# Low part of K on all 128 partitions, and a bfloat16 identity and mask, in the scores of a forgetting-attention layer

## The chip, the cores and the metric

One NeuronCore of one Trainium2 chip runs the whole program in one launch. The metric is the device time of that core in microseconds (us). Three runs of the kernel before gave a median of 2899.41 us (2898.84 to 2900.05).

## The reference, cut to what matters

A trunk of two layers over x of 1024 tokens by 1024 channels in float32: a short gated convolution beside a Mamba-2 scan, a convolutional FFN, a forgetting attention, and a second FFN, each followed by a layer norm. The change lies in the attention alone (16 heads of 64 channels, 1024 tokens):

```python
log_f = log_sigmoid(f_logit + b_f); cum = cumsum(log_f)
def block(q_blk, cum_blk, i):                 # 128 queries
    s = q_blk @ k.T * 64**-0.5 + cum_blk[..., None] - cum[:, :, None, :]
    s = where(key_pos <= qpos, s, -inf)
    p = softmax(s)
    return p @ v
```

## The kernel before, in words

Every float32 operand of a large product is held as the sum of two float32r parts, high and low, made by `split` (L95 to L98): ScalarE copies the high part, VectorE subtracts it from the source. A product takes three passes (high high, high low, low high).

`attention` (L520) handles the heads in eight pairs. The projections to q, k and v (`projections`, L610) run 24 units of 2 halves with 24 products of 512 columns each (L621), in steps of four products. Each finished half is evacuated beside the next one (`evacuations`, L572). For one head of a pair, q is a tile of 128 partitions: the high part of its 64 channels on one half of the partitions, the low part on the other (L603, L604). `kh` holds the high part of K on both halves (the split at L599 and the copy at L600), so that one product with 128 rows gives q high times k high plus q low times k high. `kl`, the low part of K, holds both heads of a pair in one tile, each on its own 64 partitions.

`scores` (L646) then makes, for 128 queries (tile i) and the (i + 1) * 128 keys up to them, in one accumulation in PSUM: the products with `kh` (128 rows), those with `kl` (64 rows), each in pieces of up to 512 keys, and one product of the identity with a mask that adds 1e38 above the diagonal (L660, 128 columns). VectorE adds the cumulated gates and takes the minimum (L663), ScalarE the exponential (L666), VectorE the reciprocal (L667), GpSimd the scaling (L668). `weigh` (L671) transposes the probabilities (L682) and splits them; `values` (L688) multiplies by v (L698), and adds the two halves of the result with a copy `ot` by ScalarE (L701) and an add by VectorE (L702).

The order: the loop at L771 goes over the 128 tiles of scores; the transposes follow two tiles, the values four tiles behind, and between them `fill` takes steps of the projections (and for the last pair, steps of the output projection, L729). Tile pools give each tag a number of slots: `kl` 2, `kh` 3, `q` 3, `vc` 1 (the copy of v before its transposes, L586, L589), `ot` 2. `places_of` (L746) names slots that come free at the end for parts of the output projection. The framework orders the instructions and places the waits.

Of the kernel before, what the change touches and what calls it, by code (L numbers as in the profile page):

```python
# [18 lines left out]
P = 128  # L19
L = 1024  # L20
# [9 lines left out]
LAG, VLAG = 2, 4    # tiles of 128 tokens by which the transposes and P @ V follow the scores  # L30
XLAG = 2            # tiles by which the transposes into x.T follow the layer norm
LEAD = 12           # steps by which the projections run ahead of the heads
FILL, FILL7 = 36, 72  # steps of products between the heads of a pair, and of the last pair


class Net:
    """The trunk. Every float32 operand of a large product is held as the exact sum of
    two float32r parts, high and low; a product takes the passes hh, hl and lh."""
# [56 lines left out]
    def split(self, high, low, src, engine=None):  # L95
        """high + low == src exactly."""
        self.nc.scalar.copy(high, src)  # L97
        (engine or self.nc.vector).tensor_sub(low, src, high.bitcast(F32))  # L98
# [19 lines left out]
    def project(self, *srcs):  # L118
        """[128 channels, L] = W[:, 128 channels].T @ x.T for each slice of W; several go
        side by side over the rows of x.T."""  # L120
        nc = self.nc
        ws = [src if isinstance(src, (tuple, list)) else self.weight(src) for src in srcs]
        ps = [self.mm_ps() for _ in srcs]
        steps = [(half, k, t, n) for k in range(KD) for t in range(len(srcs)) for n in range(3) for half in range(2)]
        if self.fresh > 0:
            self.fresh -= len(srcs)
            steps.sort(key=lambda s: s[0])
        for half, k, t, n in steps:
            if half:
                while self.after:  # L130
                    self.after.pop(0)()
            h, l = ws[t]
            w, x = ((h, self.xh), (h, self.xl), (l, self.xh))[n]
            hs = slice(half * 512, half * 512 + 512)
            nc.tensor.matmul(ps[t][:, hs], lhsT=w[:, k * P:(k + 1) * P], rhs=x[:, k, hs],  # L135
                             start=(k == 0 and n == 0), stop=(k == KD - 1 and n == 2))
        return ps if len(srcs) > 1 else ps[0]

    def conv(self, out, ps, w, bias=None):
        """Causal depthwise convolution along the free axis; w[:, K] by channel."""  # L140
        nc = self.nc
        K = w.shape[-1]
        if bias is None:
            nc.scalar.activation(out, ps, AF.Copy, scale=w[:, K - 1:K])
        else:
            nc.scalar.activation(out, ps, AF.Identity, scale=w[:, K - 1:K], bias=bias)  # L146
        for s in range(1, K):
            nc.vector.scalar_tensor_tensor(out=out[:, s:], in0=ps[:, :L - s], scalar=w[:, K - 1 - s:K - s],  # L148
                                           in1=out[:, s:], op0=ALU.mult, op1=ALU.add)

    def down(self, ys, ws, evac, late=0):
        """evac(i, psum) for each tile i of 128 tokens of y @ W; what it returns is called after the
        products of the next tile or, after the last tiles, beside the next projection. The last ones
        of ys may come late."""
        nc = self.nc
        n = len(ys)
        blocks = [range(3)] + [[i] for i in range(3, NT)] if late else [[i] for i in range(NT)]
        after = self.after
        for block in blocks:
            ps = {i: self.mm_ps() for i in block}  # L160
            for js in (range(n - late), range(n - late, n)):
                for i in block:
                    for j in js:
                        (yh, yl), (wh, wl) = ys[j], ws[j]
                        for m, (y, w) in enumerate(((yh, wh), (yh, wl), (yl, wh))):
                            for hs in (slice(0, 512), slice(512, D)):
                                nc.tensor.matmul(ps[i][:, hs], lhsT=y[:, i * P:(i + 1) * P], rhs=w[:, hs],  # L167
                                                 start=(j == 0 and m == 0), stop=(j == n - 1 and m == 2))
            while len(after) > XLAG - 1:
                after.pop(0)()  # L170
            after += [then for then in [evac(i, ps[i]) for i in block] if then]

    def log1p_exp_neg_abs(self, x, tmp):
        """log1p(exp(-|x|)) / 2, by 2 atanh(e / (2 + e))."""
# [19 lines left out]
    def thin_weight(self, src, into):  # L194
        """The 16 columns of W as the first of 128, the others zero."""
        nc = self.nc
        raw = self.wp.tile([P, KD, P], F32, tag="wraw", name="wraw", bufs=2)
        nc.gpsimd.memset(raw, 0.0)
        nc.sync.dma_start(raw[:, :, :NH], src)
        self.split(*into, raw.rearrange("p k c -> p (k c)"))  # L200
        return into

    def token_major_16(self, ps, t):
        """[128, (tile of 128 tokens, 16)] from [16 channels, L]; t: [128, L] of scratch."""
        nc = self.nc
        nc.scalar.copy(t[:NH], ps[:NH])
        tp = self.sm_ps()
        for i in range(NT):
            nc.tensor.transpose(tp[:, i * NH:(i + 1) * NH], t[:NH, i * P:(i + 1) * P], self.ident[:NH, :NH])
        return tp  # L210

# [7 lines left out]
    def layer_norm(self, r, ps, rsum, lg, lb, spare=None):  # L219
        """In place on r[128 tokens, D], with its sums over D; ps is free for scratch."""  # L220
# [74 lines left out]
    def mixer0(self):  # L295
# [17 lines left out]
        with ExitStack() as s1:  # L313
            cq = s1.enter_context(tc.tile_pool(name="cq", bufs=1))
            xs = [self.rp.tile([P, D], F32, tag=f"r{c}", name=f"xs{c}") for c in range(NT)]
            with ExitStack() as s2:
# [5 lines left out]
                # dt and the decays, [128 steps, chunk, head]  # L322
# [30 lines left out]
                # x, B, C  # L353
# [73 lines left out]
                # gated short convolution, with the scan beside it  # L427
# [14 lines left out]
            # gate  # L442
# [31 lines left out]
            # output projection  # L474
# [45 lines left out]
    def attention(self, r_in):  # L520
# [8 lines left out]
        with tc.tile_pool(name="fox", bufs=1) as fp:  # L529
# [7 lines left out]
            maskr = fp.tile([P, P], F32R, name="maskr")  # L537
            V.tensor_copy(maskr, mask)
            identr = fp.tile([P, P], F32R, name="identr")
            V.tensor_copy(identr, self.ident)  # L540
            # cumulative log forget gates
# [30 lines left out]
            def evacuations(pr, kind, n, ps):  # L572
                """Half n of the projection in its bank, as the operands of the heads 2 pr and 2 pr + 1."""
                h = half[n]
                if n == 0:
                    if kind == "v":
                        tiles["vc"] = fp.tile([P, L], F32, tag="vc", name="vc", bufs=1)
                        tiles[pr, "v"] = fp.tile([P, NT, 2, P], F32R, tag="v", name="v", bufs=2)
                    elif kind == "k":
                        tiles[pr, "kl"] = fp.tile([P, L], F32R, tag="kl", name="kl", bufs=2)  # L580
# [3 lines left out]
                if kind == "v":  # L584
                    vc, v = tiles["vc"], tiles[pr, "v"]
                    nc.scalar.copy(vc[:, h], ps)  # L586
                    yield
                    for c in range(4):
                        nc.tensor.transpose(ps[:, c * P:(c + 1) * P], vc[:, (4 * n + c) * P:(4 * n + c + 1) * P], self.ident)  # L589
# [6 lines left out]
                for e, (a, b) in enumerate(sides):  # L596
                    if kind == "k":
                        kh, kl = tiles[pr, "kh"][e], tiles[pr, "kl"]
                        self.split(kh[a, h], kl[a, h], ps[a])  # L599
                        nc.scalar.copy(kh[b, h], ps[a])  # L600
                    else:
# [8 lines left out]
            def projections():  # L610
                """All of q, k and v, in steps of a few products, each half evacuated beside the next."""
# [34 lines left out]
            def scores(pr, e, i):  # L646
                q, kh, kl = [tiles[pr, kind] for kind in ("q", "kh", "kl")]
                n = (i + 1) * P
                ts = slice(i * P, n)
                es = slice(e * 64, e * 64 + 64)  # L650
# [5 lines left out]
                for m, (a, k) in enumerate(((q[e], kh[e]), (q[e][es], kl[es]))):  # L656
                    for bs in parts:
                        nc.tensor.matmul(wide[:, bs], lhsT=a[:, ts], rhs=k[:, bs], start=(m == 0),  # L658
# [29 lines left out]
            def values(pr, e, g):  # L688
# [11 lines left out]
                ot = fp.tile([64, 256], F32, tag="ot", name="ot", bufs=2)  # L700
# [10 lines left out]
            def output_projection():  # L711
                """alpha x + o @ W of the heads 0 to 7 on x_d, in steps of a few products."""
# [33 lines left out]
            def places_of(j):  # L746
                """Slots for the parts of y and W of pair j that the last projections and heads leave free."""
# [4 lines left out]
                elif j == 5:  # L752
                    v = fp.tile([P, 2, L], F32R, tag="v", name="late", bufs=2)
                    t = [own("kl", 2), own("vc", 1), v[:, 0], v[:, 1]]
                elif j == 6:
                    t = [own("q", 3), own("kh", 3)] + weights()
                else:
                    t = [own("p", 4), own("p", 4), own("kl", 2), own("q", 3)]
# [34 lines left out]
            # the rest of the output projection  # L793
# [33 lines left out]
def _inputs(a):  # L827
    """The arrays as the chip reads them: tiles of 128 rows or columns, each contiguous."""
# [57 lines left out]
```

## Time and profile before

| | |
|---|---|
| median of 3 runs | 2899.41 us |
| span of the profiled execution, first to last instruction | 2901.4 us |
| PE busy | 2867.8 us (99%), 13378 matmuls |
| DVE busy | 1525.6 us (53%) |
| ACT busy | 918.5 us (32%) |
| POOL busy | 173.0 us (6%) |

PE is the matmul engine, PEld its weight loads, DVE VectorE, ACT ScalarE, POOL GpSimd. The page gives no other time of the profiled execution than its span; it lies 2.0 us above the median of the runs. Matmuls are pipelined and the end of each is modelled, so a matmul's duration holds more than the time by which it moves the next one; what a matmul takes of the engine is read here from the start of one to the start of the next.

### The profile page before, as it was taken

What the parts mean: (1) busy time and instruction counts of PE and PEld (TensorE: products, weight loads), DVE (VectorE), ACT (ScalarE), POOL (GpSimd) and SP (SyncE); (2) the same over time, 40 slices, a digit from 0 to 9 for tenths busy, and PEclk for the clock granted to TensorE, in tenths of its full rate; (3) what the DMA queues carried; (4) which work ended last, traced back from release to release, by engine and by line L of the source; (5) the groups of instructions that cost most, each with busy time, mean ns of one, the idle gap of its engine ahead of it and who ended that gap; (6) DMA issues with size and microseconds to landing.
All of it is one profiled execution on the core that took longest, in us unless ns stands there. A gap on an engine that the chain in (4) does not pass through costs nothing.

```text
span 2901.4 us, 32466 instructions
## 1 busy us (share of the span) xinstructions
PE 2867.8 (99%) x13378; PEld 2328.2 (80%) x13378; DVE 1525.6 (53%) x2085; ACT 918.5 (32%) x1346; POOL 173.0 (6%) x176
## 2 busy tenths in 40 slices
PE   8999999999999999999999999999899999999998
PEld 7888888888788888888887777777687888888887
DVE  4545564444644444554475555555575444444446
ACT  4521111321322222222235555555333222222222
POOL 0000000000000000000002222222100000000000
PEclk9999999999999999999999999999999999999999
DMA  3112221352011111111111111111532111111111
GB/s 136 44 66 81 75 78 66 131 189 87 22 51 56 57 48 51 51 44 44 59 73 53 52 52 44 45 44 51 182 124 73 44 44 44 51 52 57 51 37 73
DMA packets 56771, 194.50 MB, mean 67 GB/s; under 512 B 9392, under 2 KB 9776, under 8 KB 56624
## 3 DMA queue, kind: packets, MB, share of 16 engines
q1 hardware_dynamic: 56624, 192.44, 18.8%
q8 instruction: 105, 1.72, 0.2%
q14 instruction: 42, 0.34, 0.0%
HBM read 167.64 MB, written 24.77 MB: 66 GB/s over the span
## 4 chain that ended last, share of the span: by engine, by line
PE 91%; DVE 5%; ACT 1%; DMA 1%; issue 1%; POOL 0%; SPq 0%; POOLq 0%; ACTq 0%; DVEq 0%
PE mm L135 50%; PE mm L167 20%; PE mm L621 8%; PE mm L658 3%; PE sm L698 3%; PE sm L682 2%; PE mm L660 1%; PE sm L403 1%; PE mm L729 1%; DVE r L230 1%; DVE r L227 1%; DVE s L663 1%; ACT mm L226 1%; PE sm L414 0%; PE sm L409 0%
## 5 line engine op out<-in xcount | busy, mean ns | idle before, releaser
L135 PE MATMUL mm<-xh,wh 128*128 128x512 f32 x2112 | 667.7, 393 | 9.0 <-ACT xh L97 6.9
L135 PE MATMUL mm<-xh,wl 128*128 128x512 f32 x2112 | 663.0, 391 | 0.1
L135 PE MATMUL mm<-xl,wh 128*128 128x512 f32 x2112 | 661.4, 391 | 0.0
L98 DVE TENSOR_TENSOR wl<-wraw,wh 128x1024 fp32r<-128x1024 f32 x217 | 265.4, 1224 | 643.1 <-ACT wh L97 642.6
L97 ACT CAST wh<-wraw 128x1024 fp32r<-128x1024 f32 x217 | 228.0, 1051 | 1123.2 <-PE mm L135 927.3
L135 PEld LDWEIGHTS mm<-xh,wh 128*128 128x128 f32 x2112 | 395.6, 188 | 96.4 <-ACT xh L97 7.8
L135 PEld LDWEIGHTS mm<-xh,wl 128*128 128x128 f32 x2112 | 396.8, 188 | 86.2 <-issue 2.9
L135 PEld LDWEIGHTS mm<-xl,wh 128*128 128x128 f32 x2112 | 397.3, 188 | 84.8 <-issue 1.7
L282 DVE SCALAR_TENSOR_TENSOR r<-r,mm 128x1024 f32<-128x1024 f32 x160 | 195.0, 1219 | 134.1 <-PE mm L167 130.4
L167 PE MATMUL mm<-wh,yh 128*128 128x512 f32 x832 | 260.0, 392 | 0.3
L167 PE MATMUL mm<-wl,yh 128*128 128x512 f32 x832 | 256.8, 390 | 0.0
L167 PE MATMUL mm<-wh,yl 128*128 128x512 f32 x832 | 256.2, 389 | 0.0
L148 DVE SCALAR_TENSOR_TENSOR ug<-mm,ffn_cw,ug 128x1022 f32<-128x1022 f32 (+1 forms) x176 | 224.3, 1277 | 10.8 <-ACT ug L146 9.2
L167 PEld LDWEIGHTS mm<-wh,yh 128*128 128x128 f32 x832 | 153.9, 188 | 36.3 <-issue 5.1
L167 PEld LDWEIGHTS mm<-wh,yl 128*128 128x128 f32 x832 | 156.2, 188 | 32.7
L167 PEld LDWEIGHTS mm<-wl,yh 128*128 128x128 f32 x832 | 156.1, 188 | 32.6
L668 POOL TENSOR_TENSOR s<-s,sum 128x128 f32<-128x128 f32 (+7 forms) x128 | 147.8, 1155 | 459.0 <-DVE sum L667 412.0
L621 PE MATMUL mm<-xh,wh 128*128 128x512 f32 x384 | 159.1, 414 | 0.0
L621 PE MATMUL mm<-xh,wl 128*128 128x512 f32 x384 | 158.0, 412 | 0.0
L621 PE MATMUL mm<-xl,wh 128*128 128x512 f32 x384 | 154.4, 402 | 0.0
L663 DVE CUSTOM_DVE_ANT_0 s<-mm,cb 128x128 f32<-128x128 f32 (+7 forms) x128 | 96.5, 754 | 77.5 <-PE mm L660 61.1
L98 DVE TENSOR_TENSOR p<-sm,p 128x512 fp32r<-128x512 f32 (+1 forms) x192 | 105.5, 554 | 35.8 <-ACT p L97 33.9
(225 smaller groups left out, 2937.3 us busy)
## 6 DMA issues: line engine op xcount, KB each, us to landing
wraw<-in_ffn_w_up SPq DMA_DIRECT2D x88, 512.0 KB, 3.4
wraw<-in_sc_ssm_w_in SPq DMA_DIRECT2D x44, 512.0 KB, 3.5
wraw<-in_ffn_w_down SPq DMA_DIRECT2D x44, 512.0 KB, 3.4
wraw<-in_fox_w_in SPq DMA_DIRECT2D x24, 512.0 KB, 3.4
R<-acs_d SPq DMA_DIRECT2D x16, 512.0 KB, 3.6
wraw<-in_sc_ssm_w_out SPq DMA_DIRECT2D x16, 512.0 KB, 3.8
cb<-cum_d SPq DMA_DIRECT2D x16, 512.0 KB, 3.6
xraw<-in_xT SPq DMA_DIRECT2D x8, 512.0 KB, 9.3
```

The costliest lines, as they stand in the source:

```text
L97: self.nc.scalar.copy(high, src)
L98: (engine or self.nc.vector).tensor_sub(low, src, high.bitcast(F32))
L135: nc.tensor.matmul(ps[t][:, hs], lhsT=w[:, k * P:(k + 1) * P], rhs=x[:, k, hs], start=(k == 0 and n == 0), stop=(k == KD - 1 and n == 2))
L148: nc.vector.scalar_tensor_tensor(out=out[:, s:], in0=ps[:, :L - s], scalar=w[:, K - 1 - s:K - s], in1=out[:, s:], op0=ALU.mult, op1=ALU.add)
L167: nc.tensor.matmul(ps[i][:, hs], lhsT=y[:, i * P:(i + 1) * P], rhs=w[:, hs], start=(j == 0 and m == 0), stop=(j == n - 1 and m == 2))
L282: nc.vector.scalar_tensor_tensor(out=r[i], in0=r[i], scalar=ALPHA if first else 1.0, in1=ps, op0=ALU.mult, op1=ALU.add, **({"accum_out": r ...
L621: nc.tensor.matmul(place, lhsT=a[:, k * P:(k + 1) * P], rhs=x[:, k, half[n]], start=(m == 0), stop=(m == KD * 3 - 1))
L658: nc.tensor.matmul(wide[:, bs], lhsT=a[:, ts], rhs=k[:, bs], start=(m == 0), stop=(m == 1 and bs.stop < n))
L663: V.tensor_tensor_reduce(out=s[:, :n], in0=wide[:, :n], in1=cb[:, :n], op0=ALU.add, op1=ALU.min, scale=1.0, scalar=3e38, accum_out=mn)
L668: nc.gpsimd.tensor_tensor(s[:, :n], s[:, :n], sm.broadcast_to([P, n]), op=ALU.mult)
L682: nc.tensor.transpose(tp[:, c * P:(c + 1) * P], s[:, (b + c) * P:(b + c + 1) * P], self.ident)
L698: nc.tensor.matmul(ops[:, cs], lhsT=v[:, j, e, :], rhs=pt[j // 4 * 2 + m][:, j % 4, cs], start=(j == 0 and m == 0), stop=(j == 2 * g + 1 a ...
```

## The change

- `kl` becomes one tile for each head, with the low part on both halves of the partitions: the half with the head's channels is written as before, and a further ScalarE copy (64 partitions by 512) takes it to the other half. The product with it has 128 rows, with the same stationary q as that with `kh`. The tag has 3 slots in place of 2.
- The identity and the mask of the diagonal are bfloat16 in place of float32r.
- The copy of v before its transposes has 512 columns in place of 1024, and `ot` takes its slot (one slot for both, in place of one and two).
- `places_of` takes two `kl` slots for pair 5 (before: one and `vc`).

Comments and docstrings are also taken out.

```diff
-            maskr = fp.tile([P, P], F32R, name="maskr")
+            maskr = fp.tile([P, P], BF16, name="maskr")
-            identr = fp.tile([P, P], F32R, name="identr")
+            identr = fp.tile([P, P], BF16, name="identr")
...
-                        tiles["vc"] = fp.tile([P, L], F32, tag="vc", name="vc", bufs=1)
...
-                        tiles[pr, "kl"] = fp.tile([P, L], F32R, tag="kl", name="kl", bufs=2)
+                        tiles[pr, "kl"] = [fp.tile([P, L], F32R, tag="kl", name="kl", bufs=3) for _ in range(2)]
...
-                    vc, v = tiles["vc"], tiles[pr, "v"]
-                    nc.scalar.copy(vc[:, h], ps)
+                    vc, v = fp.tile([P, 512], F32, tag="vc", name="vc", bufs=1), tiles[pr, "v"]
+                    nc.scalar.copy(vc, ps)
...
-                        kh, kl = tiles[pr, "kh"][e], tiles[pr, "kl"]
+                        kh, kl = tiles[pr, "kh"][e], tiles[pr, "kl"][e]
                         self.split(kh[a, h], kl[a, h], ps[a])
                         nc.scalar.copy(kh[b, h], ps[a])
+                        nc.scalar.copy(kl[b, h], kl[a, h].bitcast(F32))
...
-                for m, (a, k) in enumerate(((q[e], kh[e]), (q[e][es], kl[es]))):
+                for m, k in enumerate((kh, kl)):
                     for bs in parts:
-                        nc.tensor.matmul(wide[:, bs], lhsT=a[:, ts], rhs=k[:, bs], start=(m == 0),
+                        nc.tensor.matmul(wide[:, bs], lhsT=q[:, ts], rhs=k[:, bs], start=(m == 0),
...
-                ot = fp.tile([64, 256], F32, tag="ot", name="ot", bufs=2)
+                ot = fp.tile([64, 256], F32, tag="vc", name="ot", bufs=1)
...
-                    t = [own("kl", 2), own("vc", 1), v[:, 0], v[:, 1]]
+                    t = [own("kl", 3), own("kl", 3), v[:, 0], v[:, 1]]
...
-                    t = [own("p", 4), own("p", 4), own("kl", 2), own("q", 3)]
+                    t = [own("p", 4), own("p", 4), own("kl", 3), own("q", 3)]
```

## Rows read from the trace of the kernel before

**Rows 1.** The page: span, and granted TensorE clock in 40 slices.
```profile
span 2901.4 us, 32466 instructions
...
PEclk9999999999999999999999999999999999999999
```

**Rows 2.** The chain that ended last, shares of the span by engine.
```profile
PE 91%; DVE 5%; ACT 1%; DMA 1%; issue 1%; POOL 0%; SPq 0%; POOLq 0%; ACTq 0%; DVEq 0%
```

**Rows 3.** Busy us (instructions) by engine, clock, DMA: one pair; late in the last.
```profile
1579.75:1648.33 68.58, 68.33 (x371) 53.22 (x370) 40.38 (x94) 39.62 (x84) 18.38 (x16) 1.00 0.14 47
...
2060.00:2080.00 20.00, 16.10 (x78) 12.16 (x77) 8.76 (x17) 4.62 (x8) 0.83 (x1) 1.00 0.67 212
```

**Rows 4.** PE in order of time over one head: start us, us, line, operation.
```profile
1705.48 0.22 PE L658 MATMUL mm<-kh,q 128*128 128x128 f32 x1
1705.63 0.32 PE L658 MATMUL mm<-kl,q 64*128 64x128 f32 x1
1705.88 0.33 PE L660 MATMUL mm<-maskr,identr 128*128 128x128 f32 x1
1706.04 0.45 PE L621 MATMUL mm<-xh,wh 128*128 128x512 f32 x1
1706.33 0.40 PE L621 MATMUL mm<-xl,wh 128*128 128x512 f32 x1
1706.56 0.40 PE L621 MATMUL mm<-xh,wl 128*128 128x512 f32 x1
...
1708.63 0.36 PE L658 MATMUL mm<-kh,q 128*128 128x256 f32 x1
...
1709.43 0.63 PE L682 MATMUL sm<-ident,s 128*128 128x128 f32 x4
...
1711.39 0.33 PE L658 MATMUL mm<-kh,q 128*128 128x384 f32 x1
1711.65 0.44 PE L658 MATMUL mm<-kl,q 64*128 64x384 f32 x1
1712.02 1.63 PE L698 MATMUL sm<-p,v 128*128 128x256 f32 x12
1713.48 0.27 PE L660 MATMUL mm<-maskr,identr 128*128 128x128 f32 x1
1713.59 0.30 PE L682 MATMUL sm<-ident,s 128*128 128x128 f32 x1
...
1714.66 0.40 PE L658 MATMUL mm<-kh,q 128*128 128x512 f32 x1
...
1715.58 0.41 PE L682 MATMUL sm<-ident,s 128*128 128x128 f32 x2
...
1719.56 0.45 PE L658 MATMUL mm<-kh,q 128*128 128x512 f32 x2
...
1720.59 0.51 PE L682 MATMUL sm<-ident,s 128*128 128x128 f32 x3
...
1733.26 0.62 PE L658 MATMUL mm<-kh,q 128*128 128x512 f32 x2
...
1734.64 0.62 PE L682 MATMUL sm<-ident,s 128*128 128x128 f32 x4
```

**Rows 5.** Weight loads in order of time, same stretch; idle time before in brackets.
```profile
1705.62 0.18 PEld L658 LDWEIGHTS mm<-kl,q 64*128 64x128 f32 x1 [0.19 <-issue]
...
1706.33 0.19 PEld L621 LDWEIGHTS mm<-xh,wl 128*128 128x128 f32 x1
```

**Rows 6.** The copy of K's high part (L600): ns min/median/max, first and last start.
```profile
L600 ACT CAST kh<-mm x32: 577/582/587, 1528.5 to 2011.9; 64x512 fp32r<-64x512 f32 x32
```

**Rows 7.** Waits from 1470 to 2110 us: total us, times, longest.
```profile
ACT kh L600 <- DVE kl L98: 18.7, 25, 1.4
...
PEld sm L698 <- DVE p L98: 8.4, 17, 1.6
```

**Rows 8.** The copies of tile ot, in the same columns.
```profile
L701 ACT COPY ot<-sm x64: 369/369/373, 1555.7 to 2121.0; 64x256 f32<-64x256 f32 x64
```

More of the change, by code (lines that the diff above doesn't have):

```diff
@@ L584, in evacuations @@
                 if kind == "v":
-                    vc, v = tiles["vc"], tiles[pr, "v"]
-                    nc.scalar.copy(vc[:, h], ps)
+                    vc, v = fp.tile([P, 512], F32, tag="vc", name="vc", bufs=1), tiles[pr, "v"]
+                    nc.scalar.copy(vc, ps)
                     yield
                     for c in range(4):
-                        nc.tensor.transpose(ps[:, c * P:(c + 1) * P], vc[:, (4 * n + c) * P:(4 * n + c + 1) * P], self.ident)
+                        nc.tensor.transpose(ps[:, c * P:(c + 1) * P], vc[:, c * P:(c + 1) * P], self.ident)
                     tv = ps.rearrange("p (c e d) -> p c e d", c=4, e=2)
@@ L646, in scores @@
             def scores(pr, e, i):
-                q, kh, kl = [tiles[pr, kind] for kind in ("q", "kh", "kl")]
+                q, kh, kl = [tiles[pr, kind][e] for kind in ("q", "kh", "kl")]
                 n = (i + 1) * P
                 ts = slice(i * P, n)
-                es = slice(e * 64, e * 64 + 64)
                 if i == 0:
```

## The prediction

> **What bounds the kernel now.** I read the page first, then the chain of waits, the busy time by stretch, and the matmul engine in order of time. The page shows a span of 2901.4 us and the clock at its upper level in nearly every slice [rows 1]. The chain of what ended last lies on PE for 91% of the span [rows 2]. In the attention, whose score tiles are all that the change touches, one pair of heads takes 68.58 us, PE is busy for 68.33 of them, and DVE and ACT for 40.38 and 39.62 [rows 3]. So in this stage any time by which PE gets on sooner shortens the kernel, until another engine's chain comes late; ACT has some 29 us a pair to spare. The exception is the last pair: late in it PE is busy for 16.10 of 20.00 us and the DMA engines for 0.67 of the time [rows 3]. There transfers set part of the pace.
>
> A matmul's worth has to be read from start to start. In the projections' stream one with 512 columns and 128 rows takes 0.23 us (1706.33 to 1706.56) [rows 4]. Its weight load does not add to that: the load for the matmul of 1706.56 starts at 1706.33, together with the matmul before it [rows 5]. With 256 columns the product with v takes about 0.12 us (twelve in 1.46 us, from 1712.02 to 1713.48, two of them of 128 columns) [rows 4]. I take 0.175 for 384 columns, half way, as an estimate. With 128 columns, the mask's product takes 0.11 us where it stands between products of 128 rows (1713.48 to 1713.59) [rows 4].
>
> **The change part by part.** *The product with K's low part on 128 rows.* Now it has 64 rows, and around it the steps are long. In tile 0 of the head shown, high part to low part takes 0.15 us, low part to mask 0.25, and mask to the next product 0.16, for three matmuls of 128 columns that cost 0.11 each elsewhere [rows 4]. The weight load of the low part starts at 1705.62, beside its own matmul and not beside the one before, after 0.19 us in which PEld waited for nothing that the profile shows [rows 5]. Going from 128 rows to 64 and back thus costs a stall on the way in and one on the way out. With all three products on 128 rows I expect the steps of the stream. For each tile, from the first product with the high part to the product behind the mask [rows 4]:
> - tile 0: 0.56 us now (1705.48 to 1706.04); three of 0.11 = 0.33 after; gains 0.23.
> - tile 1: 0.80 (1708.63 to 1709.43); 0.12 + 0.12 + 0.11 = 0.35; gains 0.45.
> - tile 2, where the products with v stand ahead of the mask: its two steps are 0.26 + 0.37 = 0.63; two of 0.175 = 0.35; gains 0.28. Its mask is already among products of 128 rows.
> - tile 3: 0.92 (1714.66 to 1715.58); 0.23 + 0.23 + 0.11 = 0.57; gains 0.35.
> - tile 4: 1.03 (1719.56 to 1720.59); 0.23 + 0.11 + 0.23 + 0.11 + 0.11 = 0.79; gains 0.24.
> - tile 7: 1.38 (1733.26 to 1734.64); four of 0.23 and 0.11 = 1.03; gains 0.35.
> - tiles 5 and 6 at the mean of tiles 4 and 7: 0.30 each.
>
> That is 2.50 us a head and 40.0 us for 16 heads. The first seven pairs give 35.0 us. Of the last pair's 5.0 us I count 3.5: its first head runs as the others do, but part of the second waits for transfers, and a wait for a transfer grows by what PE saves ahead of it.
>
> A rule of the Trainium skill speaks against part of this. The page "TensorE: Matmul & The Clock Gate", in Part 3 under "The mechanism", says that a weight load runs beside matmuls in flight only where the two use different row groups. By it the low part's products would go on paying for their loads on 128 rows; with the same page's time for a load of 128 columns, 107 ns ("LDWEIGHTS"), their 192 pieces would keep an estimated 20.5 us of the gain. The trace does not agree, since the projections' loads lie beside matmuls on the very same rows [rows 5].
>
> I keep the stream's step; what would come of the low part's loads staying in the open is rival 4.
>
> *Identity and mask as bfloat16.* No row shows a bfloat16 matmul. At best its step falls to 0.055 us, an estimate from the stream's slope (0.23 - 0.12 us for 256 columns more, half of it for 128) [rows 4]; that is 128 times 0.055 = 7 us more gain. At worst PE stalls when the type changes as it does now when the rows change: 0.25 + 0.16 us around the mask in tile 0 against 0.22 [rows 4], so 0.19 us a tile and 24 us of the gain back. I take the 0.11 us that the same product shows between others of 128 rows, the nearest row, since what follows it must load its weights all the same.
>
> *The further ScalarE copy.* There are 32 of them, like the copy at L600: 0.58 us each, 18.6 us in all, 2.3 us a pair [rows 6]. L600 already waits 18.7 us in 25 of its turns for VectorE's subtraction of the low part, which is just what the new copy reads [rows 7]; so the new one finds its data there. ACT would go from 39.6 of 68.6 us to about 42 of 64. At nothing, then, by ACT's free time. If that cover fails, up to 18.6 us come onto the path, since ACT works in order and the exponentials and the copies of the probabilities stand behind it. PE waits 8.4 us in 17 turns for VectorE's part of those probabilities today [rows 7]. I add 1 us to these waits and to those of the new slots.
>
> *Slots.* `kl` with three slots turns over like `kh`, for the same scores, so it adds no later release. `ot` and the copy of v now share one slot. `ot` is held for a copy of 0.37 us and an add, 64 times over 565 us, so about once in 9 us [rows 8]; 16 copies of v must find a place between them. Either can wait for the other for a microsecond or two on ACT; behind it stand the exponential and the probabilities of the next tiles. At nothing up to 16 times 1 us; I take it as part of the 1 us above. The late slots of pair 5 need the scores of head 14, which are done some tiles earlier; nothing.
>
> The sum: 35.0 + 3.5 - 1.0 = 37.5 us off a span of 2901.4, so 2863.9. The median of the runs lies 2.0 us under this span, so 2861.9, which I round to 2862.
>
> **The rivals.**
> 1. *The stall stays at the bfloat16 product.* PE stalls for the change of type on both sides of the mask. For it: the present stall sits just there, and nothing shows a mixed pair. Against: a float32 transpose follows the float32r mask at 0.11 us (1713.48 to 1713.59) [rows 4], though both are four bytes wide. The gain is 37.5 - 24 = 13.5 us: 2886.
> 2. *ACT comes late.* The copies are on the path for their whole length because PE now comes 7% sooner to whatever ACT makes. For it: values already wait for the probabilities [rows 7]. Against: ACT is free for 29 us of a pair [rows 3]. All 18.6 us lost: 2880.
> 3. *Slower.* Each evacuation of K holds ACT until VectorE's subtraction, queued behind its sum over the scores, and PE stands for the copy and the wait. It takes over 37.5 / 32 = 1.2 us of PE's time for each of 32 copies to decide so. At 0.58 for the copy [rows 6] and 1.4 for the wait, the longest that L600 has now [rows 7], it would be 63 us lost: 2925. Against: such waits exist now and PE misses only 0.25 us a pair [rows 3].
> 4. *Nothing.* The low part's loads stay in the open on 128 rows too. At 0.18 us each [rows 5], 192 of them take 35 us, and the gain of 37.5 shrinks to 2.5: about 2899. For it: they are in the open now. Against: the projections' loads are not [rows 5]. By the load time of the page named above it would be 17 us of gain, 2882.
>
> **How the numbers follow.** My forecast (gain of 33 to 47 us: 2852 to 2866) gets 0.70; rival 1 0.10, rival 2 with its half-way cases 0.12, rival 3 0.04, rival 4 0.04. The range takes the forecast, with the cheaper mask at its low end, and rival 2 up to its full price: 2851 to 2881, holding 0.82. A change under 0.2% (5.8 us) is about what a measurement here can't tell from none. Faster by more: the forecast and rivals 1 and 2, 0.92; within it: rival 4, 0.04; slower: rival 3, 0.04.
>
> **What would show it.** In the changed kernel's order of time, tile 3 of a head should take about 0.57 us from its first product to the one behind the mask, and tile 7 about 1.03; a pair about 63.5 us. Low part to mask at over 0.3 us in tile 3, or mask to next at 0.16, would show rival 1. More than 20 us of PE waiting for ACT or VectorE in the attention would show rivals 2 or 3. The low part's step at 0.33 us with 512 columns would show rival 4. I am wrong in the sum if the last pair takes all of its 5.0 us, or more, for transfers, or if the framework puts the products into another order.

## The result, and the profile after

The changed kernel takes 2856.89 us (median of 4 runs, 2855.09 to 2857.63) against 2899.26 us before: a ratio of 0.9851 with a 95% interval of 0.9837 to 0.9865, 42.4 us less. The forecast was 2862 us, 37.5 us less.

The page of the kernel after, with the lines that answer to [rows 1] and the table of busy times:

```profile
span 2853.1 us, 32454 instructions
...
PE 2818.5 (99%) x13378; PEld 2314.7 (81%) x13378; DVE 1525.8 (53%) x2085; ACT 934.5 (33%) x1378; POOL 173.0 (6%) x176
...
PEclk9999999999999999999999999999999999999999
```

As many matmuls as before; ACT has 32 instructions and 16.0 us more. Its four runs also show that a run's time is its span and 1.8 to 2.0 us more (2853.1 and 2855.09 in the profiled one).

The kernel after, busy us by engine in stretches as in [rows 3]: one pair; late in the last pair; and the whole last pair, from the mask of its first tile to its last product with v:

```profile
1593.46:1656.54 63.08, 62.52 (x371) 51.65 (x370) 40.25 (x94) 41.40 (x88) 18.35 (x16) 1.00 0.15 51
...
2014.00:2034.00 20.00, 17.99 (x90) 14.17 (x89) 9.88 (x17) 5.01 (x9) 0.65 (x1) 1.00 0.64 206
...
1974.40:2071.90 97.50, 90.06 (x499) 72.55 (x498) 62.42 (x119) 46.19 (x88) 19.85 (x17) 1.00 0.56 190
```

A pair went from 68.58 to 63.08 us, ACT in it from 39.62 to 41.40.

The kernel after, PE in order of time over a head, as in [rows 4] (the lines of the scores are L657 and L659 now, the transposes L681):

```profile
1690.61 0.22 PE L657 MATMUL mm<-kh,q 128*128 128x128 f32 x1
1690.67 0.28 PE L657 MATMUL mm<-kl,q 128*128 128x128 f32 x1
1690.78 0.23 PE L659 MATMUL mm<-maskr,identr 128*128 128x128 bf16 x1
1690.82 0.47 PE L621 MATMUL mm<-xh,wh 128*128 128x512 f32 x1
...
1693.44 0.37 PE L657 MATMUL mm<-kh,q 128*128 128x256 f32 x1
...
1693.81 0.48 PE L621 MATMUL mm<-xh,wl 128*128 128x512 f32 x1
1694.54 0.63 PE L681 MATMUL sm<-ident,s 128*128 128x128 f32 x4 [0.25 <-DVE p L98]
...
1699.17 0.40 PE L657 MATMUL mm<-kh,q 128*128 128x512 f32 x1
1699.41 0.39 PE L657 MATMUL mm<-kl,q 128*128 128x512 f32 x1
1699.64 0.23 PE L659 MATMUL mm<-maskr,identr 128*128 128x128 bf16 x1
1699.70 0.39 PE L681 MATMUL sm<-ident,s 128*128 128x128 f32 x2
...
1716.22 0.62 PE L657 MATMUL mm<-kh,q 128*128 128x512 f32 x2
...
1717.20 0.61 PE L681 MATMUL sm<-ident,s 128*128 128x128 f32 x4
```

Tile 0 takes 0.21 us where it took 0.56, tile 1 0.37 (0.80), tile 3 0.53 (0.92), tile 7 0.98 (1.38). The low part follows the high part at 0.06 us in tile 0 and 0.24 in tile 3, and the product behind the mask comes 0.04 to 0.06 us after it. New is a transpose that starts 0.73 us after the projection ahead of it (1693.81 to 1694.54), where a step is 0.23.

Weight loads of the kernel after, in order of time, as in [rows 5]:

```profile
1690.61 0.19 PEld L657 LDWEIGHTS mm<-kl,q 128*128 128x128 f32 x1
1690.78 0.10 PEld L659 LDWEIGHTS <-identr 128*128 128x128 bf16 x1
1690.78 0.20 PEld L621 LDWEIGHTS mm<-xh,wh 128*128 128x128 f32 x1
```

The low part's load now starts with the matmul before its own (1690.61). The bfloat16 load takes 0.10 us, not 0.19, and the next load starts in the same moment.

To see where a pair's time went, I added up the steps of PE, each from the start of one matmul to the start of the next and put down to the first of the two, over heads 4 to 13, and divided by the pairs. A wait is thus in the step of the matmul ahead of it, whichever that is in the kernel's order. In us a pair:

| kernel | kh | kl | mask | projections | with v | transposes | sum |
|---|---|---|---|---|---|---|---|
| before | 5.88 | 7.27 | 2.56 | 36.50 | 9.41 | 6.21 | 68.60 |
| after | 4.58 | 4.41 | 0.81 | 37.18 | 9.17 | 6.13 | 63.07 |
| rows only (below) | 4.40 | 4.38 | 1.94 | 37.13 | 9.19 | 6.16 | 63.99 |
| bfloat16 only | 6.06 | 7.33 | 0.81 | 36.70 | 9.20 | 6.04 | 66.94 |
| bfloat16, copies and slots | 6.06 | 7.33 | 0.81 | 36.69 | 9.21 | 6.04 | 66.94 |
| all scores on 64 rows | 5.91 | 5.89 | 0.81 | 37.75 | 9.23 | 6.69 | 67.24 |

(v's transposes, 0.79 us, 0.97 in the last row, are in the sum alone.)

### The profile page after: what moved, and what is told of

Its sections match the earlier page's. It is cut to its first block, busy times and chain, and to the rows that moved or that the text cites. A ratio compares the mean times of both kernels' runs of the same rounds, so it can differ in the third digit from the quotient of the medians.

```text
span 2853.1 us, 32454 instructions
## 1 busy us (share of the span) xinstructions
PE 2818.5 (99%) x13378; PEld 2314.7 (81%) x13378; DVE 1525.8 (53%) x2085; ACT 934.5 (33%) x1378; POOL 173.0 (6%) x176
## 4 chain that ended last, share of the span: by engine, by line
PE 91%; DVE 5%; ACT 2%; DMA 1%; issue 1%; POOL 0%; SPq 0%; POOLq 0%; ACTq 0%; DVEq 0%
PE mm L135 51%; PE mm L167 21%; PE mm L621 7%; PE sm L697 3%; PE mm L657 2%; PE sm L681 2%; PE mm L728 1%; PE sm L403 1%; DVE r L230 1%; DVE r L227 1%; DVE s L662 1%; DVE p L98 0%; PE sm L238 0%; DVE wl L98 0%; PE sm L414 0%
```

## The experiments

All are compared with the kernel before on the same chip, which took 2900.08 to 2902.55 us in these sessions. The changed kernel was not run again in them: a difference of a few us from its 2856.89 is one between chips, where the kernel before moved by 3.3 us (2899.26 to 2902.55).

**The kernel before, once more.** 

> The kernel before, profiled once more, because its trace had 6.8 us at the lower clock level late in the attention and its span (2901.4 us) was over the median of its runs, while the changed kernel's span was 2.0 us under its own time. If that stretch is an accident of the one execution, the span is about 2897 us, without a stretch at the lower level. If it belongs to the kernel (the last pair waits for transfers and the clock falls each time), the span is about 2901 us again, and some 3 us of the gain come from the clock.

Measured: 2900.51 us, span 2898.8. The stretch at the lower level came again, 10.2 us of it; the trace before had 6.8 us. Just ahead of it PE waits 0.84 and 0.61 us for VectorE (up to 2035.8 and 2036.7). The kernel after waits 1.17 and 0.61 us at the same place without a fall of the clock, so what makes it fall stays open. The last pair of this trace, bounded as above for the kernel after:

```profile
2011.90:2118.10 106.20, 99.72 (x499) 77.93 (x499) 61.41 (x117) 45.54 (x87) 19.17 (x16) 0.95 0.52 174
```

A granted clock of 0.95 here, 1.00 in the kernel after, whose trace has no such stretch in the attention; most of the kernels below have 3.4 or 6.8 us of it, two have none. At half speed 10.2 us hold about 5 us of delay at most, an estimate from the granted clock. Neither expectation held whole: the stretch is no accident, but the 2901.4 us of the first trace were over the median all the same.

**The change of rows alone.** Identity and mask stay float32r:

```diff
-            maskr = fp.tile([P, P], BF16, name="maskr")
+            maskr = fp.tile([P, P], F32R, name="maskr")
-            identr = fp.tile([P, P], BF16, name="identr")
+            identr = fp.tile([P, P], F32R, name="identr")
```

> The change without the bfloat16: identity and mask stay float32r. My theory: nearly all of the gain is the change of rows, and the mask costs the 0.11 us of the stream instead of the 0.04 to 0.07 us seen after, so 128 x 0.05 us = 6 us more than the changed kernel: about 2863 us (2860 to 2866). Rival: the steps around the mask owe their shortness to bfloat16 and a float32r mask keeps the 0.16 us behind it: 128 x 0.11 us = 14 us more, 2871 us. Second rival: the type is worth nothing, 2857 us.

Measured: 2866.03 us, ratio 0.9881 (0.9867 to 0.9894), so 34.0 us of gain, and a time 9.1 us over the changed kernel's. The type is worth more than the 6 us of my theory and less than the rival's 14. In the table's five pairs PE runs its 1840 products in the same order as before, so the 34.0 us come of the rows, with their copies and slots. PE in this kernel: tile 0, tile 1 of a pair's second head, and tile 3:

```profile
1724.40 0.22 PE L657 MATMUL mm<-kh,q 128*128 128x128 f32 x1
1724.46 0.27 PE L657 MATMUL mm<-kl,q 128*128 128x128 f32 x1
1724.57 0.28 PE L659 MATMUL mm<-maskr,identr 128*128 128x128 f32 x1
1724.68 0.45 PE L621 MATMUL mm<-xh,wh 128*128 128x512 f32 x1
...
1695.64 0.22 PE L659 MATMUL mm<-maskr,identr 128*128 128x128 f32 x1
1696.37 0.63 PE L681 MATMUL sm<-ident,s 128*128 128x128 f32 x4 [0.50 <-DVE p L98]
...
1733.61 0.22 PE L659 MATMUL mm<-maskr,identr 128*128 128x128 f32 x1
1733.67 0.38 PE L681 MATMUL sm<-ident,s 128*128 128x128 f32 x2
```

In tile 0 the float32r mask steps at 0.11 us between products of 128 rows, as [rows 4] had it; in tile 3 it steps at 0.06. In tile 1 of each pair's second head its step is 0.73 us, because the transposes behind it wait for VectorE; the changed kernel has this wait behind a projection. So of the table's 1.94 us for 16 masks 0.73 are that one. The other 15 take 1.21 us, against 0.77 in bfloat16. The two kernels differ by 0.92 us a pair (7.4 us for eight), and 0.44 of it are the masks' own steps. The rest lies in waits and in the order: with bfloat16 35 of the 1840 products stand elsewhere, among them the mask of tile 2, which comes right behind the low product instead of behind the products with v. No run told waits and order apart.

**bfloat16 alone**, in the kernel before (the same two lines, the other way). 

> The kernel before with only the identity and the mask in bfloat16; the low part of K stays on 64 rows. My theory: the stall into and out of 64 rows stays, and the mask saves the same 0.05 us a tile as between products of 128 rows, 6 us: about 2893 us (2890 to 2896). Rival: the mask's 0.16 us step falls to 0.05 although the stall before it stays: 14 us, 2885 us. Second rival: between 64 rows and float32r a bfloat16 product adds a stall of its own and the time rises by 5 us or more, over 2904 us.

Measured: 2888.64 us, ratio 0.9958 (0.9946 to 0.9971). The time lies between my theory's and the first rival's and is under my range; the rows show the rival's mechanism. PE in the kernel before, tile 3, low part to the product behind the mask:

```profile
1714.99 0.49 PE L658 MATMUL mm<-kl,q 64*128 64x512 f32 x1
1715.41 0.33 PE L660 MATMUL mm<-maskr,identr 128*128 128x128 f32 x1
1715.58 0.41 PE L682 MATMUL sm<-ident,s 128*128 128x128 f32 x2
```

PE in this kernel, tile 3:

```profile
1706.94 0.40 PE L621 MATMUL mm<-xh,wh 128*128 128x512 f32 x1
1707.17 0.40 PE L658 MATMUL mm<-kh,q 128*128 128x512 f32 x1
1707.50 0.50 PE L658 MATMUL mm<-kl,q 64*128 64x512 f32 x1
1707.93 0.23 PE L660 MATMUL mm<-maskr,identr 128*128 128x128 bf16 x1
1707.99 0.39 PE L682 MATMUL sm<-ident,s 128*128 128x128 f32 x2
```

High to low takes 0.33 us and low to mask 0.43, as before (0.33 and 0.42), but mask to next only 0.06 (0.17 before). In the table the masks fall by 1.75 us a pair, 14 us for eight. Both parts save time behind the mask, so their gains, 34.0 and 11.4 us, come to more than the 42.4 of both.

**The copies and slots, without their use.** The whole change, but the product reads 64 rows:

```diff
-                for m, k in enumerate((kh, kl)):
+                es = slice(e * 64, e * 64 + 64)
+                for m, (a, k) in enumerate(((q, kh), (q[es], kl[es]))):
                     for bs in parts:
-                        nc.tensor.matmul(wide[:, bs], lhsT=q[:, ts], rhs=k[:, bs], start=(m == 0),
+                        nc.tensor.matmul(wide[:, bs], lhsT=a[:, ts], rhs=k[:, bs], start=(m == 0),
```

> The whole change, copies and slots too, but the product with the low part reads only its 64 rows as before; the other half is written and not read. Against the run with bfloat16 alone it carries the cost of the 32 ScalarE copies and of the shared slots. My theory: these cost next to nothing, so it lies within 2 us of that run. Rival: ScalarE's copies reach the path for their 0.62 us each, and it lies 10 to 20 us over it; then the changed kernel has lost as much.

Measured: 2887.82 us, ratio 0.9956 (0.9943 to 0.9970), and 66.94 us a pair as in the run before, step for step. Copies and slots are hidden at this pace. Against the changed kernel this one differs in the rows of the low part's product alone, and PE's order in the table's pairs is the same: 66.94 against 63.07 us a pair, 30.9 us in all. That is the rows by themselves. The steps of `kh` and `kl` give 4.40 us a pair, and the projections' steps take 0.49 of it back. Whether copies and slots are hidden at the changed kernel's pace too, three more runs ask.

**The copy on GpSimd** (`nc.gpsimd.tensor_copy` for the added copy). 

> The changed kernel with the copy of the low part to the other half on GpSimd in place of ScalarE. In the changed kernel the projections' steps hold 0.68 us a pair more waiting than before, 5.4 us in all. My theory: this comes from PE reaching VectorE's work sooner, and the copies have no part in it: 2857 us, within 2. Rival: the copies on ScalarE make it, and it goes with them: about 2851 us. Second rival: GpSimd's copy is slow and shares ports with VectorE: over 2860 us.

Measured: 2857.85 us, ratio 0.9853 (0.9837 to 0.9870), 63.08 us a pair, no step of the table changed by more than 0.01. The theory held: taken off ScalarE the copy gives nothing back.

**Its own slot for `ot`** (`tag="ot"`, bfloat16). 

> The changed kernel with a slot of its own for the copy of the values' second half (in bfloat16, so that it fits the memory), apart from the copy of v. In the changed kernel the copy of v waits 4.2 us in 7 turns for VectorE to leave this slot. My theory: this is ScalarE's own slack and the time stays, 2857 us within 2. Rival: ScalarE's delay is on the path: 4 us less, 2853 us.

Measured: 2858.18 us, ratio 0.9853 (0.9838 to 0.9868), 63.08 us a pair. The shared slot costs nothing.

**Each copy twice.** 

> The changed kernel with each copy of the low part made twice on ScalarE: 32 more of 0.62 us, 20 us of work. My theory: ScalarE is busy for 41 of 63 us a pair and hides it; up to 3 us more, 2857 to 2860 us. Rival: the copies are on the path: 20 us more, 2877 us.

Measured: 2861.97 us, ratio 0.9867 (0.9853 to 0.9882): 5 us more than the changed kernel and about 4 more than the two runs before it, which are of the same session; over my 3 and far under 20. ACT is busy for 43.47 of 64.00 us (this kernel, one pair):

```profile
1586.00:1650.00 64.00, 62.84 (x370) 51.85 (x369) 40.43 (x94) 43.47 (x92) 18.35 (x16) 1.00 0.14 50
```

What the second copy itself costs is not shown. The framework ordered this kernel's PE anew: 95 of the table's 1840 products stand elsewhere. PE's weight loads now wait 1.7 us in 7 turns for ScalarE's `kh`, which the changed kernel's don't, so part of it may be the copies.

**The product with v one tile later** (`LAG, VLAG = 2, 5`). 

> The changed kernel with the product with v five tiles behind the scores in place of four. In the changed kernel that product waits about 0.40 us twice a pair for VectorE's split of the probabilities, and a transpose 0.5 us once. My theory: these waits are what the change has brought nearer or left, and one tile more of distance takes away the 0.8 us a pair before the product with v: about 6 us less, 2851 us. Rival: VectorE's queue is then late for the next thing instead, and the time stays at 2857 us.

Measured: 2860.19 us, ratio 0.9860 (0.9845 to 0.9875): 3 us more than the changed kernel and 2 more than the runs with the copy on GpSimd and with a slot of its own, which are of the same session; a miss. The weight loads' wait ahead of the product with v shrank (6.1 us in the kernel after), but the next scores now wait for VectorE's sum (0.2 in the kernel after). Waits of the weight loads from 1530 to 1970 us in this kernel:

```profile
PEld mm L657 <- DVE mn L662: 3.5, 7, 0.5
...
PEld sm L697 <- DVE p L98: 1.5, 7, 0.2
```

**VectorE relieved.** The low parts of the projections' weights go to GpSimd:

```diff
+                                self.low_engine = nc.gpsimd
                                 ready = self.weight(win[work[u + 1][2]])
+                                self.low_engine = nc.vector
```

> The changed kernel with the low parts of the projections' weights subtracted on GpSimd in place of VectorE (23 subtractions of 1.22 us each, three a pair, leave VectorE). My theory: what the changed kernel waits for in the attention is VectorE's queue (1.3 us a pair at three places, the split of the probabilities behind such subtractions); one of the three stands right behind a subtraction and goes, 0.5 us a pair, 4 us in all: 2853 us. Rival: GpSimd takes longer and holds VectorE at the shared ports or delays its own scaling of the probabilities: over 2860 us.

Measured: 2857.51 us, ratio 0.9849 (0.9834 to 0.9864): no less in all, so the number was a miss. But a pair takes 62.67 us, and the projections' steps fall from 37.18 to 36.68, which is near the 36.50 of before. The wait of 0.50 us ahead of the transposes is down to 0.14: they now stand behind a mask, whose step is 0.20 where it is 0.07 without a wait. One pair of this kernel, and that place:

```profile
1660.20:1722.87 62.67, 62.37 (x371) 51.70 (x369) 36.92 (x91) 41.40 (x88) 25.45 (x20) 1.00 0.15 51
...
1694.93 0.23 PE L661 MATMUL mm<-maskr,identr 128*128 128x128 bf16 x1
1695.13 0.63 PE L683 MATMUL sm<-ident,s 128*128 128x128 f32 x4
```

In the two profiled executions (spans 2853.1 and 2856.0 us) the 2.1 us that seven pairs gave (445.5 to 443.4) were lost again: 1.3 us ahead of the first mask (1528.9 to 1530.2), and 3.7 us in the last pair (97.5 to 101.2). The last pair took 97.5, 99.8 and 100.9 us in the changed kernel and in the runs with the copy on GpSimd and with a slot of its own, which have the same pairs; so most of the 3.7 us may be scatter. Whether GpSimd's subtractions meet anything in either place, no run told apart.

**Both together.** 

> The run before it and the product with v five tiles behind the scores. With VectorE relieved, the wait of the next scores for VectorE's sum, which made the later product with v cost 3 us, should shrink: by my theory 1.3 us a pair less waiting in all than in the changed kernel, 2847 us. Rival: the order of the products themselves makes the waits, and it stays over 2857 us.

Measured: 2863.52 us, ratio 0.9869 (0.9853 to 0.9886), 63.89 us a pair. My theory fell: with VectorE relieved, the later product with v costs 6.0 us against the run before it. The scores' wait for VectorE's sum is hardly less (3.1 us in 8 turns in place of 3.5 in 7). What else the later product costs by, no run shows.

**Everything on 64 rows.** The products with the high part also read 64 rows (`q[e][es], kh[e][es]`), in the kernel with bfloat16 alone. 

> The kernel before with the mask in bfloat16 and both products of the scores on 64 rows; q low times k high is left out. It tells apart what the stall hangs on. Theory A: on the change of rows, two changes a tile as in the run with bfloat16 alone, and the time stays there, 2889 us. Theory B: on each product with 64 rows, whose weight load is not beside the matmul before it, and on the load behind the last: then one more boundary in tiles 0 to 3 and two more in tiles 4 to 7, 192 in all, of 0.10 us each, 19 us more, about 2908 us; a second piece of the high part would follow the first at 0.33 us in place of 0.23.

Measured: 2889.79 us, ratio 0.9961 (0.9946 to 0.9975): theory A's time. PE in this kernel, tile 3 and then tile 7:

```profile
1676.29 0.40 PE L621 MATMUL mm<-xh,wh 128*128 128x512 f32 x1
1676.62 0.50 PE L658 MATMUL mm<-kh,q 64*128 64x512 f32 x1
1676.95 0.39 PE L658 MATMUL mm<-kl,q 64*128 64x512 f32 x1
1677.28 0.23 PE L660 MATMUL mm<-maskr,identr 128*128 128x128 bf16 x1
...
1695.34 0.74 PE L658 MATMUL mm<-kh,q 64*128 64x512 f32 x2
1695.92 0.63 PE L658 MATMUL mm<-kl,q 64*128 64x512 f32 x2
1696.48 0.23 PE L660 MATMUL mm<-maskr,identr 128*128 128x128 bf16 x1
```

The step into the 64 rows is 0.33 us (1676.29 to 1676.62), the first one within them 0.33, the one out 0.33; further ones run at the stream's pace: in tile 7 the four pieces take 0.58 and 0.56, that is 0.34 + 0.24 and 0.23 + 0.33 by the trace's single starts. So a run of 64-row products costs three times 0.10 us in runs of two and of four, and 64 rows as such cost nothing. A run of one pays about as much: in tile 3 above 0.33 and 0.43 us, each against 0.23. The second piece at 0.33 was theory B's mark, but what follows it was not.

**A version from these.** GpSimd for the weights' low parts in the middle pairs alone (`if 2 <= u < 20`). 

> The changed kernel with the low parts of the projections' weights on GpSimd only for units 3 to 20 of 24 (the weights of the second to the seventh pair), since the run with all of them there took 62.67 us a pair in place of 63.07 but lost 2 us in the first pair and 4 us in the last. My theory: the pairs keep their 62.7 us and the ends are those of the changed kernel: 7 times 0.4 = 3 us less, 2854 us. Rival: the last pair loses the same again because its order follows from the pairs before: 2857 us.

Measured: 2854.64 us, ratio 0.9839 (0.9825 to 0.9852), 62.83 us a pair. It is the fastest median, but its interval overlaps the changed kernel's, so it is not shown to beat it. In the profiled executions seven pairs gave 1.5 us (445.5 to 444.0) and the last pair took 1.9 more (97.5 to 99.4).

## Why the prediction was right, and which sizes were off

The mechanism was right and the time lay 5 us under the forecast, inside the range, by errors of both signs, so that the number is closer than its terms.

- *The rows.* The sum put high and low products at 8.76 us a pair after the change (the steps of its list, with tiles 5 and 6 by the same steps, twice the eight tiles without the mask); 8.99 was measured, and 8.78 with float32r. The list's steps of the stream held. The three stalls that a run of 64 rows costs (the experiment with everything on 64 rows) are what went; I had counted two, but the sums over whole tiles already held the third. The products with v and the transposes took 0.32 us a pair less, which I had not counted.
- *The mask*, the term that was mis-sized. I took 0.11 us, the step of float32r, "since what follows it must load its weights all the same"; it is 0.05 on average, my best case. 16 masks at 0.06 us less are 0.95 us a pair and 7.6 us in all. Even for float32r 0.11 was too much: with the rows alone six of a pair's 16 masks step at 0.11 and nine at 0.06. In bfloat16 the load lasts 0.10 us in place of 0.19 and the next load starts beside it. Rival 1, a stall at the change of type, is refuted by the same rows: low part to mask takes 0.23 us in tile 3 and mask to next 0.06.
- *The waits.* I took 1 us in all for new ones. The projections' steps, which hold most of them, grew by 0.68 us a pair, 5.4 us. I had looked for them as delays of ScalarE; the runs with the copy on GpSimd and with a slot of its own show that neither has a part in them. 0.50 us of the 0.68 are one wait a pair for VectorE's queue, which PE reaches sooner; where the other 0.18 lie, no line here shows. In the kernel after:

```profile
1691.66 1.22 DVE L98 TENSOR_TENSOR wl<-wraw,wh 128x1024 fp32r<-128x1024 f32 x1 [0.21 <-ACT wh L97]
...
1692.99 0.69 DVE L604 SCALAR_TENSOR_TENSOR q<-mm,q 64x512 fp32r<-64x512 f32 x1
1693.70 0.69 DVE L98 TENSOR_TENSOR p<-sm,p 128x512 fp32r<-128x512 f32 x1
```

  The split that ends at 1694.39 stands behind a weight's subtraction and q's, and the transposes at 1694.54 wait for it. With the subtraction on GpSimd this wait fell to 0.14 us.
- *The copies and slots* cost nothing, as forecast. In the kernel after, the instructions of the added copy's line, as in [rows 6] (count, then lowest, median and highest ns of one):

```profile
L600 ACT CAST kl<-kl x32: 614/618/622, 1528.1 to 1973.3; 64x512 fp32r<-64x512 f32 x32
```

  and its waits from 1470 to 2070 us, as in [rows 7] (us waited, turns, the longest):

```profile
PEld sm L697 <- DVE p L98: 10.1, 17, 1.8
...
ACT kh L599 <- DVE kl L98: 8.1, 11, 1.4
...
ACT vc L585 <- DVE o L701: 4.2, 7, 0.6
```

  A copy takes 0.62 us, not the 0.58 of L600 before. ACT's own wait for the subtraction fell from 18.7 to 8.1 us [rows 7], the weight loads' for the probabilities rose from 8.4 to 10.1, and the copy of v (`vc`) waits 4.2 us for the add that frees its shared slot, with no loss in the time. How much room was left is not shown: with a second copy of 2.5 us a pair the time rose by 4 to 5 us, but PE's order was another too. Rivals 2 and 3 did not come: PE misses 0.56 us of a pair (63.08 less 62.52) where it missed 0.25. Nor did rival 4: the low part follows at 0.24 us in tile 3, where 0.33 would have shown it.
- *The ends.* The first seven pairs gave 39.4 us (first mask to that of the last pair: 1528.9 to 1974.4 against 1527.0 to 2011.9 in the second trace of before), where I had 35.0; the last pair gave 8.7 (106.2 to 97.5) where I had 3.5. These are single executions and add to 48.1 us, where the medians differ by 42.4: the one of the kernel after is its fastest, 1.8 us under its median, and 1.9 us went ahead of the first mask (1527.0 to 1528.9). In the runs with the copy on GpSimd and with a slot of its own, of the same 63.08 us a pair, the last pair gave 6.5 and 5.3. The lower clock level, which I had not counted although the first trace showed it, may be up to 5 us of the 8.7. But the first trace, with 3.4 us less of it, took 106.5 for the last pair, so its share is not shown; how often it comes in either kernel stays open.
- *The span.* I read the 2.0 us between the span and the median as an offset. A run's time lies 1.7 to 2.1 us over its span in all runs here, so the first profiled execution took about 2903.3 us (an estimate), 4 us over the median. The forecast of the median is the same either way.
- *A rule on weight loads.* The weight loads of the kernel after lie beside matmuls on the same 128 rows (the load of 0.19 us at 1690.61 above), and in a run of 64-row products the steps are the stream's from the third on (0.23 to 0.24 us). The rule weighed in the prediction, of the Trainium skill's page "TensorE: Matmul & The Clock Gate" (Part 3, "The mechanism"), that a load runs beside matmuls only where the row groups differ, does not hold here.

## What to carry to other kernels

Look at the rows of neighbouring matmuls before their count: on a bound PE a short run of 64-row products among 128-row ones cost 31 to 34 us here, and the copies that filled the other half cost nothing that shows, on ScalarE or on GpSimd. Read matmuls from start to start, in the order of time; the busy share of PE was 99% before and after. In a table of steps, look for the waits before you price an operation: one of 16 masks held more than a third of their time. And where a change lets the framework order the products anew, compare the orders before you put a few us down to the change. When PE gets faster, ask which queue it now reaches too early, and test the obvious suspect by taking it away: here it was not the engine that got the new work.

## What was not expected of the hardware

- A run of 64-row products pays 0.10 us on entry, at the second product and on exit, and none between: in the run with everything on 64 rows, pieces of 512 columns step at 0.33, 0.33 or 0.34 and then 0.23 to 0.24 us.
- A bfloat16 matmul of 128 columns between float32r ones steps at 0.04 to 0.07 us (0.06 to 0.11 for float32r in its place) and its load lasts 0.10 us against 0.19. It ends an accumulation of float32r products, and no stall shows there: the step into it is 0.11 us in tile 0 and 0.23 in tile 3, as with a float32r mask.
